# Six raw weight buffers, modulation tiles loaded one ahead, and half of layer 0's w_in multiplied without a split

## The chip, the core and the metric

The kernel runs on one core of a Trainium2 chip. TensorE (PE, with its weight loads listed as PEld) does the matrix products, VectorE (DVE), ScalarE (ACT) and GpSimd (POOL) the rest, and SyncE (SP) issues nearly all transfers from HBM. The metric is the device time of one execution in microseconds, the median over several runs.

## What is computed

Two layers of an encoder over 256 tokens of 2048 features, all in float32. Only what bears on the change is shown:

```
c_act = silu(c)                                   # (1, 2048)
for l in range(2):
    mod = c_act @ ada_w[l] + ada_b[l]             # 6 parts of 2048: sh1 sc1 g1 sh2 sc2 g2
    h = rmsnorm(x, norm_mix_g[l]) * (1 + sc1) + sh1
    proj = h @ w_in[l] + b_in[l]                  # 2048 -> 5392
    y = concat(RG-LRU, attention, hyena, mLSTM of slices of proj)
    x = x + g1 * (y @ w_out[l])                   # 2048 -> 2048
    h = rmsnorm(x, norm_ffn_g[l]) * (1 + sc2) + sh2
    x = x + g2 * ((silu(h @ ffn_w1[l]) * (h @ ffn_w3[l])) @ ffn_w2[l])   # 2048 -> 5632 -> 2048
return rmsnorm(x, final_g)
```

## The kernel before

Features lie on partitions, tokens on the free axis: the stream `x` is 16 row tiles of 128 features by 256 tokens. A weight matrix is read in *pieces* of 128 x 1024 floats (512 KB): four row tiles of a pair of 128-column blocks. w_in has 21 pairs, so 84 pieces, and 2 pieces more for the gates; w_out has 64, w1 and w3 together 176, w2 96 (some of 384 KB).

**Exact products out of fast passes.** The type F32R lets TensorE run a float32 product in one pass of reduced precision. To lose nothing, every weight piece and every activation tile is split into `hi` (ScalarE copies and rounds, L335) and `lo` (VectorE subtracts, L336), and `product` issues three matmuls per row tile and column block: hi by hi (L372), hi by lo (L373), lo by hi (L374). An activation tile `h` is made by `norm`'s `make(k)`: a tiny gain `g` (L493), `x` times gain times 1/rms (L495), the shift on ScalarE with rounding to hi (L497), and lo on VectorE (L498).

**Buffers.** `_load` brings pieces into `NRAW` = 3 raw tiles, `_split` makes `NHL` = 3 pairs of hi and lo. `fetch`, called ahead of each piece, loads and splits up to those numbers ahead of the piece in use. A raw tile is free again after its split.

**Modulation.** `mod` is a matrix-vector product that VectorE does: `ada` loads half a column block of ada_w (128 x 1024 floats, 512 KB) and multiplies and sums it in one instruction (L423), into `acc`; after the second half a tiny sum with the bias follows (L428, 128 x 1), or, for the parts g1 and g2, two for the whole part (L432, L433). There are 384 such halves. `RATES` says how many halves are worked on per weight piece: 1 in layer 0's w_in, less later, none after layer 1's w_out. `modc` computes on until a wanted column is there. The 64 halves that the first norm needs are worked through during the start, between the steps of `spectra` (the long filters of the hyena mixer, in full float32 products), with up to six tiles in flight; later halves have `NADA` = 2 tiles.

**Order.** A list scheduler orders the instructions of each engine at build time, from the program's order, priorities and its own timing; on the chip every engine and the SP queue run strictly in that order. `load` keeps a transfer behind the last weight load that the program asked for before it. The first `IN_LEAD` = 4 pairs of w_in are worked on together, chunk by chunk of four row tiles, as `h` comes into being; later pairs one after the other. The same holds for w_out (5 pairs) and w1/w3 (3 pairs).

Of the kernel before, what the change touches and what calls it, by code (L numbers as in the profile page):

```python
# [18 lines left out]
P = 128  # L19
DEPTH = 2  # L20
# [24 lines left out]
def _in_columns():  # L45
    """Source column of every column of the 42 plain blocks, in the kernel's order."""
# [33 lines left out]
# ---------------------------------------------------------------- constants of the shapes  # L80
def _constants():
# [36 lines left out]
    # behind the permutation of the rotation: rows 2 i and 2 i + 1 spread over the halves of tile i  # L118
# [38 lines left out]
# ---------------------------------------------------------------- layout of the inputs  # L157
# [67 lines left out]
# ---------------------------------------------------------------- the program  # L225
# pairs of column blocks that are worked on together while their input is still being made
IN_LEAD, OUT_LEAD, FFN_LEAD = 4, 5, 3
# half columns of the modulation per piece of weights, by layer: w_in, first w1 and w3, the rest of the FFN, w_out
# [3 lines left out]
class Lazy:  # L232
    """A list of n tiles, each made when it is first asked for, in their order."""
# [13 lines left out]
class Net:  # L247
    NRAW, NHL, NADA = 3, 3, 2
    # 2 KB tiles, by what they hold: a tag's tiles get their places in the order of the program
# [71 lines left out]
    def _load(self):  # L321
        ap, n = self.items[self.n_dma]
# [5 lines left out]
    def _split(self):  # L328
        k = self.n_split
        n = self.items[k][1]  # L330
        t = self.raw.pop(k)
        with self.tc.high_priority(offset=1500):
# [5 lines left out]
        self.n_split += 1  # L338
# [17 lines left out]
    def product(self, banks, acts, m):  # L356
        """bank[:, b*T:(b+1)*T] = W[:, block b].T @ act, for m blocks of 128 columns in each bank.
        acts: per row tile, [hi | lo]. Several banks take turns chunk by chunk."""
# [3 lines left out]
        for done in range(0, nk, per):  # L362
            use = [acts[done + i] for i in range(min(per, nk - done))]
            for ps in banks:
                hi, lo = self.next_weights()
                for i, a in enumerate(use):
                    for b in range(m):
# [3 lines left out]
                        last = done + i == nk - 1  # L371
                        mm(o, hi[:, c], a[:, :T], start=first and b == 0, stop=False, skip_group_check=True)  # L372
# [4 lines left out]
    def products(self, n, lead, acts):  # L377
        """The banks of n pairs of column blocks in turn; the first `lead` of them are worked on together."""
# [8 lines left out]
    def split(self, dst, src):  # L387
        """dst (float32r) = [hi | lo] of src, exactly."""
# [4 lines left out]
    def ada_init(self, order):  # L393
# [11 lines left out]
        self.acc = [self.cp.tile([P, 96, 2], F32, name=f"acc{l}") for l in range(DEPTH)]  # L405
        self.ada_items = [(l, b, h) for l, b in order for h in range(2)]
        self.ada_at = 0
        self.ada_left = 0.0

    def ada(self, n, wide=False):  # L410
        """The next n half columns of the modulation; wide: with more of them under way."""
        nc = self.nc
        self.ada_left += n
        while self.ada_left >= 0.999 and self.ada_at < len(self.ada_items):
            self.ada_left -= 1
            l, b, h = self.ada_items[self.ada_at]
            self.ada_at += 1
            if wide and self.ada_at % 3:
                t = self.pair("ad")
            else:  # L420
                t = self.wp.tile([P, 1024], F32, tag="ada", name=self.nm("ada"), bufs=self.NADA)
            self.load(t, self.d["ada"][l, b, :, h * 1024:(h + 1) * 1024])
            nc.vector.scalar_tensor_tensor(t, t, 1.0, self.cb[:, h * 1024:(h + 1) * 1024], ALU.mult, ALU.mult,  # L423
                                           accum_out=self.acc[l][:, b, h:h + 1])
            if h == 0:
                continue
            if b // 16 not in (2, 5):
                nc.vector.scalar_tensor_tensor(self.mod[l][:, b:b + 1], self.acc[l][:, b, 0:1], self.acc[l][:, b, 1:2],  # L428
                                               self.pc(l, "ada_b", b), ALU.add, ALU.add)
            elif b % 16 == 15:  # L430
                m = self.mod[l][:, b - 15:b + 1]
                nc.vector.tensor_tensor(m, self.acc[l][:, b - 15:b + 1, 0], self.acc[l][:, b - 15:b + 1, 1], ALU.add)  # L432
                nc.vector.tensor_tensor(m, m, self.pc(l, "ada_b", b - 15, 16), ALU.add)  # L433

    def modc(self, l, j, k):
        """Column k of part j; parts 2 and 5 come as a whole."""
        b = j * 16 + k
        while self.ada_at <= self.ada_items.index((l, b | 15 if j in (2, 5) else b, 1)):
            self.ada(1, wide=l == 0 and j < 2)
        return self.mod[l][:, b:b + 1]  # L440

# [1 line left out]
    def rsqrt(self, v, n):  # L443
        """v ** -0.5 of a tiny tile: a start from ScalarE, one Newton step on it."""
# [40 lines left out]
    def norm(self, l, gname, jsh, jsc):  # L485
# [3 lines left out]
        def make(k):  # L489
            sc, sh = self.modc(l, jsc, k), self.modc(l, jsh, k)  # L490
            with self.tc.high_priority(offset=50):
                g = self.yp.tile([P, 1], F32, tag="g", name=self.nm("g"))
                nc.vector.scalar_tensor_tensor(g, sc, 1.0, self.pc(l, gname, k), ALU.add, ALU.mult)  # L493
                t = self.tmp("h")
                nc.vector.scalar_tensor_tensor(t, self.x[k], g, rb, ALU.mult, ALU.mult)  # L495
                h = self.slot("h", F32R)
                nc.scalar.activation(h[:, :T], t, AF.Identity, bias=sh)  # L497
                nc.vector.scalar_tensor_tensor(h[:, T:], t, sh, h[:, :T].bitcast(F32), ALU.add, ALU.subtract)  # L498
# [13 lines left out]
    def sine(self, ps, b, sf):  # L512
        """sin(sf * (ps + b)) of 64 rows, the argument brought into [-pi, pi] first."""
# [16 lines left out]
    def filters(self):  # L530
        """The hidden layers of the networks of the long filters."""
# [13 lines left out]
    def spectra(self, h):  # L545
        """Spectra of the long filters, without their norm, into DRAM; the norms per channel into self.rs."""
# [13 lines left out]
    def third(self, l):  # L560
        """Last weights of the filters' network, the decays below those of the first quarter."""
# [7 lines left out]
    def early(self, n):  # L569
        """Modulation and first norm, between the steps of the spectra."""  # L570
        self.ada(min(n, 64 - self.ada_at), wide=True)
# [76 lines left out]
    def taps(self, src, dst, w, b, left):  # L648
        """Depthwise convolution over the tokens; w: columns of the taps."""
# [9 lines left out]
    def hyena(self, l, hf, pv, dft, spec, rs):  # L659
        """One half (two tiles) of the channels; pv: projections of v, x1, x2."""  # L660
# [58 lines left out]
    def attention(self, l, pq, pkv):  # L719
        """pq: two pairs of q tiles (heads i and i + 4 in tile i); pkv: k tile | v tile."""  # L720
# [395 lines left out]
    def weight_items(self):  # L1116
# [9 lines left out]
        def pairs(aps, lead, k0=0, k1=KT):  # L1126
            put(aps[:lead], k0, k1)
            for ap in aps[lead:]:
                put([ap], k0, k1)
# [58 lines left out]
```

## Time and profile before

| | |
|---|---|
| median of 3 runs | 2657.58 us (2656.99 to 2659.11) |
| span of the profiled execution | 2648.9 us; its own time is not listed, and the runs' times lie 8.1 to 10.2 us above this span |
| mean granted TensorE clock | 0.972 |
| PE busy | 2523.5 us (95%), 19410 matmul records |
| DVE busy | 1811.4 us (68%) |
| ACT busy | 1158.7 us (44%) |
| moved by DMA | 630.19 MB, mean 238 GB/s |

Times in the rows below are microseconds from the start of the span unless marked ns. A full float32 product appears as two weight loads and two matmul records, an F32R pass as one of each. Matmuls overlap in the pipeline, so what one costs is read from how closely the starts follow each other, not from its own length. Roughly, the start lasts until 175 us, layer 0's w_in with the mixers until 545, w_out until 627, the FFN until 1409; layer 1's w_in with the mixers until 1790, w_out until 1865, its FFN until 2636.

### The profile page before, as it was taken

How to read it: one execution, taken by the hardware profiler on the slowest of the kernel's cores; microseconds unless marked ns; L12 is line 12 of the kernel's file. 1: busy time of each engine (PE TensorE's matmuls, PEld its weight loads, DVE VectorE, ACT ScalarE, POOL GpSimd, SP SyncE). 2: the span in 40 equal slices, each digit the busy share in tenths (PEclk: the TensorE clock that was granted, in tenths of full speed). 3: DMA queues.
4: the chain of work that ended last, by engine and by line, in shares of the span. 5: the costliest groups of instructions: out<-in, count | busy, mean ns of one | idle time of the engine just before them, and what ended most of it. 6: DMA issues, size and time to landing. Idle time of an engine off the chain costs nothing.

```text
span 2648.9 us, 47579 instructions
## 1 busy us (share of the span) xinstructions
PE 2523.5 (95%) x19410; PEld 2404.3 (91%) x19410; DVE 1811.4 (68%) x2778; ACT 1158.7 (44%) x1669; POOL 161.9 (6%) x142
## 2 busy tenths in 40 slices
PE   6889989798999999999998999999899999999998
PEld 3469989598999999999998898989899999999998
DVE  7888788778767666766677767777766454454445
ACT  4444455444443344334434445654444334433443
POOL 2101010021000000000020111002000000000001
PEclk9789999898999999999999999999999999999999
DMA  8787878467887778887776766658688656556654
GB/s 281 267 308 267 263 255 295 173 244 241 278 281 272 263 267 266 271 265 269 254 257 231 254 219 229 212 167 271 223 282 270 192 183 183 180 181 189 183 180 148
DMA packets 180752, 630.19 MB, mean 238 GB/s; under 512 B 20162, under 2 KB 20371, under 8 KB 180531
## 3 DMA queue, kind: packets, MB, share of 16 engines
q1 hardware_dynamic: 177076, 620.84, 70.5%
q10 hardware_dynamic: 3456, 6.29, 0.6%
q8 instruction: 152, 2.49, 0.4%
q14 instruction: 68, 0.56, 0.1%
HBM read 618.67 MB, written 8.39 MB: 237 GB/s over the span
## 4 chain that ended last, share of the span: by engine, by line
PE 58%; DMA 8%; DVE 5%; issue 4%; ACT 1%; SPq 0%; POOL 0%; DVEq 0%; POOLq 0%; ACTq 0%
PE a L374 19%; PE a L373 19%; PE a L372 19%; DMA ada<-in_ada 6%; DVE lo L336 2%; DMA raw<-in_w_in 1%; DMA raw<-in_w 1%; DVE ada L423 1%; ACT hi L335 0%; DMA raw<-in_w_out 0%; DVE x L1097 0%; DVE h L495 0%; DVE h L498 0%; SPq L324 0%; PE m L812 0%
## 5 line engine op out<-in xcount | busy, mean ns | idle before, releaser
L335 ACT ACTIVATE hi<-raw 128x1024 fp32r<-128x1024 f32 (+2 forms) x780 | 810.8, 1041 | 1181.4 <-PE a L373 698.5
L336 DVE TENSOR_TENSOR lo<-raw,hi 128x1024 fp32r<-128x1024 f32 (+2 forms) x780 | 948.1, 1218 | 425.1 <-ACT hi L335 419.9
L374 PE MATMUL a<-h,lo 128*128 128x256 f32 x4192 | 1204.2, 288 | 26.7 <-DVE lo L336 26.6
L372 PE MATMUL a<-h,hi 128*128 128x256 f32 x4192 | 1206.0, 288 | 10.2 <-ACT hi L335 5.5
L373 PE MATMUL a<-h,hi 128*128 128x256 f32 x4192 | 1206.3, 288 | 1.7 <-DVE h L498 1.7
L374 PEld LDWEIGHTS a<-h,lo 128*128 128x128 f32 x4192 | 815.1, 195 | 40.6 <-DVE lo L336 30.2
L372 PEld LDWEIGHTS a<-h,hi 128*128 128x128 f32 x4192 | 815.7, 195 | 28.5 <-ACT hi L335 8.9
L373 PEld LDWEIGHTS a<-h,hi 128*128 128x128 f32 x4192 | 815.5, 195 | 8.1 <-DVE h L498 2.8
L423 DVE SCALAR_TENSOR_TENSOR ada<-ada,cb 128x1024 f32<-128x1024 f32 x341 | 425.1, 1247 | 340.7 <-DMA ada<-in_ada 339.9
L374 PE MATMUL a<-g,lo 128*128 128x256 f32 x1408 | 399.7, 284 | 2.9 <-DVE lo L336 2.8
L373 PE MATMUL a<-g,hi 128*128 128x256 f32 x1408 | 399.2, 283 | 0.0
L372 PE MATMUL a<-g,hi 128*128 128x256 f32 x1408 | 399.1, 283 | 0.0
L374 PEld LDWEIGHTS a<-g,lo 128*128 128x128 f32 x1408 | 271.0, 193 | 4.0 <-DVE lo L336 4.0
L372 PEld LDWEIGHTS a<-g,hi 128*128 128x128 f32 x1408 | 271.1, 193 | 0.0
L373 PEld LDWEIGHTS a<-g,hi 128*128 128x128 f32 x1408 | 271.0, 192 | 0.0
L466 POOL TENSOR_TENSOR sq<-sq,sq 128x256 f32<-128x256 f32 x65 | 81.6, 1255 | 1694.4 <-issue 1399.7
L1097 DVE SCALAR_TENSOR_TENSOR x<-a,mod,x 128x256 f32<-128x256 f32 x128 | 55.8, 477 | 5.5 <-PE a L374 5.4
L423 DVE SCALAR_TENSOR_TENSOR ad<-ad,cb 128x1024 f32<-128x1024 f32 x43 | 54.5, 1274 | 0.1
L389 ACT ACTIVATE g<-s 128x256 fp32r<-128x256 f32 x88 | 35.9, 408 | 35.2 <-DVE s L1109 35.1
L497 ACT ACTIVATE h<-h,mod 128x256 fp32r<-128x256 f32 x64 | 29.4, 501 | 42.0 <-DVE h L495 28.5
L464 ACT ACTIVATE sq<-x 128x256 f32<-128x256 f32 x75 | 29.2, 413 | 24.5 <-DVE x L1097 24.3
L374 PE MATMUL a<-yc,lo 128*128 128x256 f32 x128 | 36.8, 288 | 1.0 <-DVE lo L336 1.0
(247 smaller groups left out, 2017.7 us busy)
## 6 DMA issues: line engine op xcount, KB each, us to landing
raw<-in_w SPq DMA_DIRECT2D x496, 512.0 KB, 4.6
ada<-in_ada SPq DMA_DIRECT2D x341, 512.0 KB, 5.7
raw<-in_w_in SPq DMA_DIRECT2D x168, 512.0 KB, 4.9
raw<-in_w_out SPq DMA_DIRECT2D x64, 512.0 KB, 5.7
ad<-in_ada SPq DMA_DIRECT2D x43, 512.0 KB, 6.3
raw<-in_w SPq DMA_DIRECT2D x32, 384.0 KB, 3.1
spectra<-sl ACTq DMA_DIRECT2D x24, 256.0 KB, 7.0
spec<-spectra SPq DMA_DIRECT2D x24, 256.0 KB, 6.7
```

Of the source, the lines that this page charges most:

```text
L335: self.nc.scalar.activation(hi[:, :n], t[:, :n], AF.Copy)
L336: self.nc.vector.tensor_tensor(lo[:, :n], t[:, :n], hi[:, :n].bitcast(F32), ALU.subtract)
L372: mm(o, hi[:, c], a[:, :T], start=first and b == 0, stop=False, skip_group_check=True)
L373: mm(o, hi[:, c], a[:, T:], start=False, stop=False, skip_group_check=True)
L374: mm(o, lo[:, c], a[:, :T], start=False, stop=last, skip_group_check=True)
L389: self.nc.scalar.activation(dst[:, :T], src, AF.Copy)
L423: nc.vector.scalar_tensor_tensor(t, t, 1.0, self.cb[:, h * 1024:(h + 1) * 1024], ALU.mult, ALU.mult, accum_out=self.acc[l][:, b, h:h + 1])
L464: nc.scalar.activation(t, self.x[k], AF.Square)
L466: nc.gpsimd.tensor_tensor(self.sq, self.sq, t, ALU.add)
L497: nc.scalar.activation(h[:, :T], t, AF.Identity, bias=sh)
L1097: self.nc.vector.scalar_tensor_tensor(self.x[k], ps[:, b * T:(b + 1) * T], g, self.x[k], ALU.mult, ALU.add)
```

## The change

- `NRAW` goes from 3 to 6. Room is made by a smaller scratch for dynamic DMAs (`dynamic_dma_scratch_size=1024`).
- `WHOLE = 8`: in layer 0, row tiles 0 to 7 of w_in and of the gates are neither split nor is their `h`: `_split` hands on the raw tile, `make` leaves `h` as plain float32 without `lo`, and `product` issues one full float32 matmul in place of three passes. That is 42 of 84 pieces and 1 of 2 for the gates. Such a raw tile is held until its matmuls are done.
- `ada` no longer loads its own half: `ada_load` asks for the tiles ahead of the one that is summed, six in the first 58 halves, `NADA` = 2 (this one and the next) after that.
- The sums with the bias are made per part (two instructions of 128 x 16) and not per column, but for the first norm; the gain `(1 + sc) * norm_g` is made beside them into a kept tile, so `make` no longer computes `g`. For this the parts come one after the other in `order`, not column by column in turn, but for the first norm.

```
-    NRAW, NHL, NADA = 3, 3, 2
+    NRAW, NHL, NADA = 6, 3, 2
+WHOLE = 8
 def _split(self):
+        self.n_split += 1
+        if whole:
+            self.hl[k] = (t, None)
+            return
 def product(self, banks, acts, m):
+                        if lo is None:
+                            mm(o, hi[:, c], a[:, :T], start=first and b == 0, stop=last, skip_group_check=True)
+                            continue
+    def ada_load(self):
+        at = self.ada_at
+        while self.ada_got < min(len(self.ada_items), at + (6 if at < 58 else self.NADA)):
+            n = self.ada_got
+            l, b, h = self.ada_items[n]
+            if n < 64 and n % 3:
+                t = self.pair("ad")
+            else:
+                t = self.wp.tile([P, 1024], F32, tag="ada", name=self.nm("ada"), bufs=self.NADA)
+            self.load(t, self.d["ada"][l, b, :, h * 1024:(h + 1) * 1024])
+            self.ada_tiles[n] = t
+            self.ada_got += 1
 def ada(self, n):
+            self.ada_load()
             l, b, h = self.ada_items[self.ada_at]
+            t = self.ada_tiles.pop(self.ada_at)
...
+            if l == 0 and j < 2:
+                m = mod[:, b:b + 1]
+                nc.vector.scalar_tensor_tensor(m, acc[:, b, 0:1], acc[:, b, 1:2], self.pc(l, "ada_b", b), ALU.add, ALU.add)
+                if j:
+                    nc.vector.scalar_tensor_tensor(self.gain[l, j][:, k:k + 1], m, 1.0, self.pc(l, "nmix", k), ALU.add, ALU.mult)
+            elif k == 15:
+                c = slice(j * 16, j * 16 + 16)
+                nc.vector.tensor_tensor(mod[:, c], acc[:, c, 0], acc[:, c, 1], ALU.add)
+                nc.vector.tensor_tensor(mod[:, c], mod[:, c], self.pc(l, "ada_b", j * 16, 16), ALU.add)
+                if j in (1, 4):
+                    nc.vector.scalar_tensor_tensor(self.gain[l, j], mod[:, c], 1.0, self.pc(l, "nmix" if j == 1 else "nffn", 0, 16),
+                                                   ALU.add, ALU.mult)
 def make(k):   # in norm
-            sc, sh = self.modc(l, jsc, k), self.modc(l, jsh, k)
+            g, sh = self.modc(l, jsc, k), self.modc(l, jsh, k)
+            whole = l == 0 and jsh == 0 and k < WHOLE
-                nc.vector.scalar_tensor_tensor(g, sc, 1.0, self.pc(l, gname, k), ALU.add, ALU.mult)
-                h = self.slot("h", F32R)
+                h = self.slot("h", F32 if whole else F32R)
                 nc.scalar.activation(h[:, :T], t, AF.Identity, bias=sh)
+                if not whole:
+                    nc.vector.scalar_tensor_tensor(h[:, T:], t, sh, h[:, :T].bitcast(F32), ALU.add, ALU.subtract)
-        order = [(l, j * 16 + k) for l in range(DEPTH) for js in ((1, 0), (2,), (4, 3), (5,)) for k in range(16) for j in js]
+        order = [(0, j * 16 + k) for k in range(16) for j in (1, 0)]
+        order += [(l, j * 16 + k) for l in range(DEPTH) for j in ((1, 0) if l else ()) + (2, 4, 3, 5) for k in range(16)]
-    nc = bacc.Bacc("TRN2", target_bir_lowering=False, num_devices=1)
+    nc = bacc.Bacc("TRN2", target_bir_lowering=False, num_devices=1, dynamic_dma_scratch_size=1024)
```

## Rows read from the trace of the kernel before

**Rows 1.** Windows by stage: length, busy us (instructions) per engine, granted clock, DMA share, GB/s.

```profile
50.00:175.00 125.00, 112.07 (x395) 66.65 (x395) 112.47 (x222) 52.18 (x105) 21.09 (x12) 0.85 0.83 297
175.00:500.00 325.00, 298.89 (x2195) 283.96 (x2195) 266.22 (x461) 159.19 (x259) 24.64 (x26) 0.96 0.80 271
...
650.00:1345.00 695.00, 694.13 (x5782) 693.73 (x5782) 477.24 (x648) 284.52 (x339) 4.28 (x3) 1.00 0.80 270
...
1425.00:1790.00 365.00, 349.54 (x2590) 326.71 (x2590) 267.26 (x470) 191.02 (x328) 27.42 (x28) 0.98 0.67 221
...
1884.00:2636.00 752.00, 751.25 (x6262) 751.17 (x6262) 406.15 (x470) 309.51 (x373) 14.47 (x13) 1.00 0.64 202
```

**Rows 2.** Waits of TensorE, 175 to 500 us: us in total, times, longest.

```profile
PE a L374 <- DVE lo L336: 16.1, 7, 7.7
```

**Rows 3.** Waits of TensorE, 1340 to 1900 us.

```profile
PE a L374 <- DVE lo L336: 10.5, 9, 3.4
PE ss L475 <- ACT sq L464: 8.4, 2, 4.8
...
PE a L372 <- ACT hi L335: 2.3, 2, 1.8
```

**Rows 4.** One window of the dense stretch of layer 0's FFN.

```profile
900.00:1000.00 100.00, 100.00 (x836) 100.00 (x835) 67.55 (x96) 42.20 (x51) 0.00 (x0) 1.00 0.81 275
```

**Rows 5.** Timeline of TensorE in layer 1's hyena: start us, us, engine, line, op, tiles, form.

```profile
1513.07 3.62 PE L684 MATMUL m<-vt,dft 128*128 128x256 f32 x16
...
1516.64 0.28 PE L372 MATMUL a<-h,hi 128*128 128x256 f32 x1
```

**Rows 6.** Windows of L374 alone: PE busy us (records), PEld busy (records), clock.

```profile
0.00:175.00 175.00, 29.05 (x84) 20.20 (x84) 0.89 0.83 291
```

**Rows 7.** Groups of VectorE, 50 to 175 us: busy us, mean ns, idle before.

```profile
L423 DVE SCALAR_TENSOR_TENSOR ad<-ad,cb 128x1024 f32<-128x1024 f32 x35 | 44.9, 1288 | 0.1
...
L336 DVE TENSOR_TENSOR lo<-raw,hi 128x1024 fp32r<-128x1024 f32 x9 | 11.7, 1297 | 3.3 <-ACT hi L335 3.3
...
L498 DVE SCALAR_TENSOR_TENSOR h<-h,mod,h 128x256 fp32r<-128x256 f32 x13 | 6.7, 516 | 4.9 <-ACT h L497 4.9
```

**Rows 8.** Groups of the whole span, by shape: VectorE.

```profile
L336 DVE TENSOR_TENSOR lo<-raw,hi 128x1024 fp32r<-128x1024 f32 x732 | 901.5, 1233 | 394.5 <-ACT hi L335 389.4 <-PE a L373 0.7 <-PE a L374 0.5
...
L428 DVE SCALAR_TENSOR_TENSOR mod<-acc,par 128x1 f32<-128x1 f32 x128 | 32.2, 252 | 1.4
...
L493 DVE SCALAR_TENSOR_TENSOR g<-mod,par 128x1 f32<-128x1 f32 x64 | 11.1, 178 | 0.3
```

**Rows 9.** Windows around three slow stretches, columns as in the first group.

```profile
182.00:190.00 8.00, 6.17 (x30) 6.17 (x31) 5.85 (x9) 1.46 (x2) 0.00 (x0) 0.57 0.52 143
353.00:364.00 11.00, 5.75 (x28) 5.75 (x29) 11.00 (x16) 2.39 (x4) 4.28 (x4) 0.53 0.40 117
...
1613.00:1624.00 11.00, 7.20 (x35) 6.79 (x35) 11.00 (x13) 2.86 (x5) 3.82 (x3) 0.53 0.36 104
```

**Rows 10.** Waits of the SP queue, whole span.

```profile
SPq L324 <- DVE lo L336: 1332.6, 574, 43.9
```

**Rows 11.** Waits of VectorE, 175 to 500 us.

```profile
DVE ada L423 <- DMA ada<-in_ada: 48.2, 36, 2.9
```

**Rows 12.** Waits of ScalarE, 590 to 627 us, the end of layer 0's w_out.

```profile
ACT hi L335 <- DMA raw<-in_w: 6.2, 3, 4.4
```

**Rows 13.** Waits of ScalarE, 1396 to 1409 us, the end of layer 0's FFN.

```profile
ACT hi L335 <- DMA raw<-in_w_in: 4.3, 2, 2.8
```

**Rows 14.** Waits of ScalarE, 1850 to 1865 us, the end of layer 1's w_out.

```profile
ACT hi L335 <- DMA raw<-in_w: 6.1, 3, 2.8
```

**Rows 15.** Waits of TensorE, 545 to 650 us.

```profile
PE ss L475 <- ACT sq L464: 3.5, 1, 3.5
```

**Rows 16.** The two DMA queues that carry data: packets, MB, share of 16 engines.

```profile
q1 hardware_dynamic: 177076, 620.84, 70.5%
q10 hardware_dynamic: 3456, 6.29, 0.6%
```

More of the change, by code (lines that the diff above doesn't have):

```diff
@@ L321, in _load @@
     def _load(self):
-        ap, n = self.items[self.n_dma]
+        ap, n, _ = self.items[self.n_dma]
         t = self.wp.tile([P, 1024], F32, tag="raw", name=self.nm("raw"), bufs=self.NRAW)
@@ L329, in _split @@
         k = self.n_split
-        n = self.items[k][1]
+        n, whole = self.items[k][1:]
         t = self.raw.pop(k)
+        self.n_split += 1
+        if whole:
+            self.hl[k] = (t, None)
+            return
         with self.tc.high_priority(offset=1500):
@@ L337, in _split @@
         self.hl[k] = (hi, lo)
-        self.n_split += 1
     def fetch(self):
@@ L405, in ada_init, with ada @@
         self.acc = [self.cp.tile([P, 96, 2], F32, name=f"acc{l}") for l in range(DEPTH)]
+        self.gain = {(l, j): self.cp.tile([P, 16], F32, name=f"gain{l}{j}") for l in range(DEPTH) for j in (1, 4)}
         self.ada_items = [(l, b, h) for l, b in order for h in range(2)]
-        self.ada_at = 0
+        self.ada_at = self.ada_got = 0
         self.ada_left = 0.0
-    def ada(self, n, wide=False):
+        self.ada_tiles = {}
+    def ada_load(self):
[10 more added lines that the diff above has]
+            self.ada_got += 1
+    def ada(self, n):
         nc = self.nc
@@ L415, in ada @@
             self.ada_left -= 1
+            self.ada_load()
             l, b, h = self.ada_items[self.ada_at]
+            t = self.ada_tiles.pop(self.ada_at)
             self.ada_at += 1
[L418 to L422, printed above, removed]
+            acc, mod = self.acc[l], self.mod[l]
@@ L423, in ada @@
             nc.vector.scalar_tensor_tensor(t, t, 1.0, self.cb[:, h * 1024:(h + 1) * 1024], ALU.mult, ALU.mult,
-                                           accum_out=self.acc[l][:, b, h:h + 1])
+                                           accum_out=acc[:, b, h:h + 1])
+            j, k = b // 16, b % 16
             if h == 0:
                 continue
[L427 to L433, printed above, removed]
+            if l == 0 and j < 2:
[10 more added lines that the diff above has]
+                                                   ALU.add, ALU.mult)
@@ L435, in modc @@
     def modc(self, l, j, k):
         b = j * 16 + k
-        while self.ada_at <= self.ada_items.index((l, b | 15 if j in (2, 5) else b, 1)):
-            self.ada(1, wide=l == 0 and j < 2)
-        return self.mod[l][:, b:b + 1]
+        while self.ada_at <= self.ada_items.index((l, b if l == 0 and j < 2 else b | 15, 1)):
+            self.ada(1)
+        return self.gain[l, j][:, k:k + 1] if j in (1, 4) else self.mod[l][:, b:b + 1]
     def rsqrt(self, v, n):
@@ L483, in rstd, with norm @@
         return pb[:, :T]
-    def norm(self, l, gname, jsh, jsc):
+    def norm(self, l, jsh, jsc):
         nc = self.nc
@@ L569, in early @@
     def early(self, n):
-        self.ada(min(n, 64 - self.ada_at), wide=True)
+        self.ada(min(n, 64 - self.ada_at))
         k = min(self.ada_at // 4, KT)
@@ L1118, in weight_items, with put @@
         d, it = self.d, []
-        def put(aps, k0, k1, w=256):
+        def put(aps, k0, k1, w=256, whole=0):
             per = 1024 // w
@@ L1123, in put, with pairs @@
                 n = min(per, k1 - k)
-                it.extend((ap[:, k:k + n, :].rearrange("p a b -> p (a b)"), n * w) for ap in aps)
-        def pairs(aps, lead, k0=0, k1=KT):
-            put(aps[:lead], k0, k1)
+                it.extend((ap[:, k:k + n, :].rearrange("p a b -> p (a b)"), n * w, k < whole) for ap in aps)
+        def pairs(aps, lead, k0=0, k1=KT, whole=0):
+            put(aps[:lead], k0, k1, whole=whole)
             for ap in aps[lead:]:
-                put([ap], k0, k1)
+                put([ap], k0, k1, whole=whole)
         for l in range(DEPTH):
             w = [d["w_in"][l, j] for j in range(21)]
-            pairs(w[:14], IN_LEAD)
-            put([d["w_gate"][l]], 0, KT, P)
-            pairs(w[14:], 1)
+            whole = 0 if l else WHOLE
+            pairs(w[:14], IN_LEAD, whole=whole)
+            put([d["w_gate"][l]], 0, KT, P, whole=whole)
+            pairs(w[14:], 1, whole=whole)
             pairs([d["w_out"][l, j] for j in range(8)], OUT_LEAD)
@@ L1153, in run @@
         self.weights(self.weight_items())
-        self.ada(4, wide=True)
-        self.h0 = h = self.norm(0, "nmix", 0, 1)
+        self.ada(4)
+        self.h0 = h = self.norm(0, 0, 1)
         self.early(4)
@@ L1161, in run @@
         for l in range(DEPTH):
-            h = h or self.norm(l, "nmix", 0, 1)
+            h = h or self.norm(l, 0, 1)
             self.rate = RATES[l][0] if l else 0
@@ L1166, in run @@
             self.add_to_stream(l, y, 2, True, OUT_LEAD)
-            h = self.norm(l, "nffn", 3, 4)
+            h = self.norm(l, 3, 4)
             self.ffn(l, h)
```

2 lines of the change are left out of this document (removed).

## Prediction, made before the changed kernel was run

> **What bounds the kernel now.** I read the windows by stage first. In both FFN stretches TensorE is busy all the time at full clock (694.1 of 695 us, 751.3 of 752), so 1447 us are bound by matmuls alone and nothing that the change does to VectorE or to transfers can shorten them. The rest is where time can come from: the start, layer 0's w_in, the norms between matrices, and layer 1's w_in and w_out [rows 1]. The busy share of TensorE flatters these stages, since a matmul that waits in the pipeline is counted. The count tells more: 2195 records in the 325 us from 175 to 500. Then I read TensorE's own waits by stage. In layer 0's w_in the largest wait is for lo, the second half of the weight split on VectorE: 16.1 us in 7 waits [rows 2]. In the 560 us around layer 1's mixer it is 10.5 us for lo and 2.3 for hi, and 8.4 us at two norms for the squares of the last row of the stream [rows 3]. VectorE is busy for 266 of those 325 us and 112 of 125 in the start [rows 1]: near full, so its queue is late whenever something else falls in.
>
> **The added cost: the unsplit products.** In the dense FFN 836 F32R passes start in 100 us, 0.1196 us each [rows 4]; a split row tile and column block is three of them, 0.359 us. A full float32 product of the same shape (128 rows, 128 columns, 256 moving) is in the hyena: sixteen records, eight products, start at 1513.07, and one F32R pass later the next start is at 1516.64; 3.57 less 0.12 is 3.45 us, 0.431 us each [rows 5]. So an unsplit product costs 0.072 us more than the three passes it replaces. There are 43 such pieces of 8 products, 344 in all: 24.9 us of TensorE time added. L374 has run 84 of its 688 times for layer 0's w_in by 175 us [rows 6], and the first eight pieces, which are all unsplit, are 64 of these: so 4.6 us fall into the start and 35 pieces, 20.3 us, into the dense part. Bounds of one product: 0.359, if it costs no more than the three passes, and 0.453, the eighth part of the 3.62 us from the first start to the last end [rows 5]; over 344 products nothing and 32 us.
>
> The Trainium skill has a rule that speaks against the change here: the page FP8 and Floating Point Precision, section TensorE Precision Notes, says that a true float32 product is four passes through the array. At the pass spacing of the FFN, weight load included, that would make 0.478 us a product and 41 us in all, and the sum below would be some 16 us higher. The row in the hyena gives 0.431, and the measurement decides.
>
> **What it removes, in the start.** VectorE no longer makes lo of eight pieces (1.297 us each, 10.4) and of eight tiles of h (0.516, 4.1) [rows 7]: 14.5 us off an engine that is busy 112 of 125 us. It stands idle for only 0.1 us before the sums on tiles of the modulation there, so it is not the loads that pace it. But TensorE also waits for the spectra and runs at a mean clock of 0.85 [rows 1], and its 4.6 us more are partly in the way. Bounds: 14.5 gained, 4.6 lost; I take 7 gained, about the middle of 14.5 and 0.
>
> **In layer 0's w_in.** Half of the pieces need neither ScalarE nor VectorE, 1.233 us of VectorE each [rows 8], 43 us of its 266. What that returns is at most the 16.1 us of waits for lo and the clock that they cost. In two windows with such waits the granted clock is 0.57 and 0.53, with 6.2 and 5.8 us busy: times the missing share, 2.7 us lost in each [rows 9]. That makes 21.5. I take 16, three quarters: the longest wait (7.7) stands behind the recurrences of the RG-LRU on VectorE's queue, which stay. Against the 20.3 us added this stage comes out 4 us longer; bounds 1 shorter and 20 longer.
>
> **Six raw buffers.** SP waits 1332.6 us for lo before it can load a piece [rows 10]: with three buffers a load goes out only once an older piece is split. Three more let each load go out three pieces earlier, 72 passes or some 8.6 us [rows 4]. In the FFN this is worth nothing. At the norms it counts: shortly before the last rows of the stream, ScalarE waits 6.2, 4.3 and 6.1 us for the next weights [rows 12 to 14], VectorE's queue stands behind it with lo, and the last update of x and its square come late; TensorE waits 3.5 and 8.4 us for them [rows 3, 15], 11.9 in all. I take 8 for the three norms; bounds 0 and 11.9. In layer 1's stages the waits for lo and hi are 12.8 us, and a half-clock window with 7.2 us busy lost 3.4 [rows 3, 9]: 16.2 at most. Some of them are queued behind activations of the recurrence and not behind loads, so I take 9; bounds 0 and 16.2.
>
> An unsplit raw tile is held until its matmuls are done, three pieces later than a split would free it; the three added buffers just pay for that. Queued behind such a load on SP are the next modulation tile and the tables of the mixers; who waits for them is VectorE, not TensorE. I cost it at nothing; without that cover it is a longer wait of VectorE of the kind that already costs 2.9 us at worst [rows 11].
>
> **Modulation loads and sums.** After the start there are two tiles for the modulation before and after, so a load still waits for the sum of two halves earlier: I expect most of VectorE's 48.2 us of waits for these tiles to stay [rows 11], and give the earlier request nothing. Removed are 96 of the 128 tiny sums with the bias (0.252 us) and 48 of the 64 gains made at their places (0.178), 33 us of VectorE [rows 8]; the 12 wide sums and three wide gains that replace them are a few us. What lies in the FFN stretches gains nothing; at the norms a tiny gain sits ahead of each of the first tiles, half a us, inside the 8 taken above. The first norm's sums stay single. The smaller scratch I cost at nothing: all data go through the two queues listed, both of the hardware kind, the same that the loads use now [rows 16]. No transfer's size or number changes.
>
> **The sum.** -7 (start) +4 (layer 0's w_in) -8 (three norms) -9 (layer 1) = -20 us against the span of 2648.9, so 2629; the median of the runs lies 8.7 above the span, which gives 2638 us. A change within 0.2%, 5.3 us, can't be told from none.
>
> **The rivals.**
> *Slower: the waits stay.* VectorE's and ScalarE's backlog in layer 0's w_in comes from the mixers, and the removed splits only leave VectorE idle. TensorE then pays the 24.9 us in full in that one stage, with the 8 of the norms returned: 2675 us. For it: waits for lo are only 16.1 of the 325 us [rows 2], and wherever there is none an unsplit product is pure loss. Against it: those waits are for the very work that is removed. It decides once less than about 20 us is recovered over the whole kernel.
> *More than forecast.* VectorE was the bound of the start after all, and the deeper loads remove every weight wait: -14.5, -1, -12, -16, together -44, 2614 us. For it: VectorE 90% busy in the start. Against: stalls behind the recurrences are not of the weights' making.
> *It comes out even.* Either an unsplit product costs four passes at the spacing of the FFN, 0.478 us and 16 us more in all than I take: 2654; the row of the hyena speaks against it, and it gets 0.05. Or the change doesn't do what it says: the earlier loads leave the splits where they were, since VectorE and not the loads set them, and of the 17 us at the norms and in layer 1 hardly any come: about 2655, with 0.09. (The rule of the Trainium skill named above is the first of these two.)
>
> **How the numbers follow.** Chances: the forecast 0.50 (its own range 2620 to 2652), more than forecast 0.20, even 0.14, slower 0.16. So faster 0.70, the same 0.14, slower 0.16. The range must hold 8 in 10: it reaches below to a little past the 2614 of the second rival and above close to the 2675 of the first, 2608 to 2672.
>
> **What would show it.** In the trace of the changed kernel: records of float32 products on `a<-h,raw` at 0.216 us spacing, 688 of them; L336 with 43 fewer groups of work; the lead pieces of w_in done some 7 us sooner; TensorE's waits for lo in layer 0's w_in down from 16 to about 4 us while that stage takes as long as before; ScalarE's waits for weights before the three norms gone, and the wait for the last square short; the FFN stretches unchanged. Wrong would be: an unsplit product at another spacing, a clock below 0.96 in w_in, or VectorE waiting longer than now for modulation tiles with TensorE behind it.

## The result

| | before | after |
|---|---|---|
| median on the same chip, 4 runs each | 2657.87 us (2656.99 to 2659.11) | 2639.76 us (2636.45 to 2642.18) |
| ratio, 95% interval | | 0.9933 [0.9917, 0.9950] |
| profiled execution: time, span | not listed, 2648.9 us | 2639.2 us, 2637.4 us |
| mean granted TensorE clock | 0.972 | 0.981 |

The change saves 18 us, where 20 were forecast. The profiled execution of after shows that a run's time lies only 1.8 us above its span. A second profile of before says the same (2660.62 and 2658.8). So the execution behind [rows 1 to 16] took about 2650.7 us, 7 below its kernel's median, and the 8.7 us that the prediction added were mostly this difference. Counted between medians the sum is not hurt; a stage read from that one execution is. The second profile of after errs the other way: its execution took 2652.61 us, the slowest of its six and 11 above their median.

The stages can be compared by the matmul `rb<-ident,v`, which starts each norm. Timeline of TensorE in after (start us, us, engine, line, op, tiles, form; in brackets the idle time before it):

```profile
29.59 0.69 PE L511 MATMUL rb<-ident,v 128*128 128x128 f32 x2 [4.04 <-DMA dft<-in_k_dft]
...
619.61 0.69 PE L511 MATMUL rb<-ident,v 128*128 128x128 f32 x2 [1.04 <-POOL v L508]
...
1407.51 0.69 PE L511 MATMUL rb<-ident,v 128*128 128x128 f32 x2 [2.37 <-POOL v L508]
...
1857.00 0.69 PE L511 MATMUL rb<-ident,v 128*128 128x128 f32 x2 [3.31 <-POOL v L508]
...
2626.87 0.43 PE L511 MATMUL rb<-ident,v 128*128 128x128 f32 x2 [1.03 <-POOL v L508]
```

The same rows of the second profile of before:

```profile
628.65 0.69 PE L482 MATMUL rb<-ident,v 128*128 128x128 f32 x2 [2.35 <-POOL v L479]
...
1419.13 0.69 PE L482 MATMUL rb<-ident,v 128*128 128x128 f32 x2 [1.85 <-POOL v L479]
...
1876.69 0.69 PE L482 MATMUL rb<-ident,v 128*128 128x128 f32 x2 [1.41 <-POOL v L479]
```

One more mark is the start of the last matmul of the 128th product of w_in, as many as the four pairs that are worked on together have; the time up to it is here called the *lead*. (In after, 7 of the 128 are already of the fifth pair, which the scheduler put ahead.) With it the span falls into stages, in us (two executions of each kernel):

| | lead | rest to the first FFN norm | layer 0's FFN | layer 1 to its FFN norm | layer 1's FFN |
|---|---|---|---|---|---|
| before | 197.6, 195.7 | 433.5, 432.9 | 781.0, 790.5 | 455.6, 457.6 | 770.4, 771.6 |
| after | 188.7, 189.1 | 430.9, 432.8 | 787.9, 785.1 | 449.5, 460.2 | 769.9, 773.0 |

Only the lead shows a difference that is larger than that between two executions of one kernel. Layer 0's FFN alone differs by 9.5 us between the two of before. The lead's difference is 8 us of the 18; by stage, the other 10 can't be told from the spread of these four executions.

The unsplit products are there, 688 records. The groups of after by line, TensorE:

```profile
L378 PE MATMUL a<-h,raw 128*128 128x256 f32 x688 | 166.6, 394 | 3.9 <-DMA raw<-in_w_in 3.9
```

128 of them lie before 175 us, the 64 products that the prediction put there. Windows of L378 alone (length, PE busy (records), PEld busy (records), clock, DMA share, GB/s):

```profile
0.00:175.00 175.00, 37.54 (x128) 27.87 (x128) 0.90 0.87 308
```

Their price is in the timeline of TensorE in after:

```profile
263.00 0.28 PE L382 MATMUL a<-h,lo 128*128 128x256 f32 x1
263.12 4.05 PE L378 MATMUL a<-h,raw 128*128 128x256 f32 x18
267.01 0.60 PE L704 MATMUL m<-ident,hn 128*128 128x128 f32 x4
```

18 records, nine products, start between 263.12 and 267.01: 0.216 us a record, 0.432 a product, as [rows 5] had it. The Trainium skill's four passes (FP8 and Floating Point Precision, TensorE Precision Notes) are in it if a pass is taken at a quarter of this, 0.108 us. The prediction's 0.478 by that rule came from taking each pass at the 0.1196 us of [rows 4]; the trace is against that price, not against the number of passes.

VectorE's splits, by shape, have 43 fewer large groups than in [rows 8]:

```profile
L342 DVE TENSOR_TENSOR lo<-raw,hi 128x1024 fp32r<-128x1024 f32 x689 | 849.5, 1238 | 348.4 <-ACT hi L341 345.1
```

Windows by stage, as in [rows 1]: from 175 to 500 VectorE is busy for 220 us, not 266.

```profile
50.00:175.00 125.00, 113.02 (x385) 66.77 (x385) 111.99 (x223) 50.13 (x102) 21.93 (x11) 0.86 0.89 318
175.00:500.00 325.00, 301.76 (x1790) 267.91 (x1790) 220.22 (x403) 121.26 (x235) 27.34 (x28) 0.97 0.74 253
```

Waits of TensorE, 175 to 500 us (total, times, longest). The 16.1 us for lo of [rows 2] are 0.9 now. What is left waits mostly for the mixers:

```profile
PE m L860 <- DVE lf L858: 8.3, 1, 8.3
PE a L380 <- ACT h L525: 3.0, 1, 3.0
...
PE a L382 <- DVE lo L342: 0.9, 1, 0.9
```

So lo was taken out of the way, but TensorE's idle time in this stretch, the length less the busy time, only went from 26.1 us [rows 1] to 23.2. The longest wait that came up, 8.3 us, stands behind a late weight piece. ScalarE, which takes its work strictly in order, waits 6.3 us for the piece and only then computes `ga`, from which VectorE makes `lf`:

```profile
376.85 1.06 ACT L341 ACTIVATE hi<-raw 128x1024 fp32r<-128x1024 f32 x1 [6.32 <-DMA raw<-in_w_in]
...
380.95 0.42 ACT L857 ACTIVATE ga<-ga 128x256 f32<-128x256 f32 x1
...
381.39 0.42 DVE L858 SCALAR_TENSOR_TENSOR lf<-gates,ga 128x256 f32<-128x256 f32 x1 [2.23 <-ACT ga L857]
...
381.88 1.11 PE L860 MATMUL m<-lf,ident 64*64 64x256 f32 x2 [8.31 <-DVE lf L858]
```

VectorE's waits for modulation tiles in the same stretch grew from the 48.2 us of [rows 11]:

```profile
DVE ada L446 <- DMA ada<-in_ada: 78.9, 49, 4.1
```

TensorE stands behind a few of them: its waits of 2.7 and 1.9 us for the hyena's `hn` come right after such a tile. The prediction had named this as a sign of being wrong. Timeline of after at the first of the two:

```profile
297.50 1.23 DVE L446 SCALAR_TENSOR_TENSOR ada<-ada,cb 128x1024 f32<-128x1024 f32 x1 [2.63 <-DMA ada<-in_ada]
...
298.65 0.48 DVE L737 SCALAR_TENSOR_TENSOR hn<-m,c,hn 128x256 f32<-128x256 f32 x1
...
299.18 0.70 PE L1029 MATMUL m<-xc,lw 128*128 128x256 f32 x2 [2.72 <-DVE hn L737]
```

### The profile page after: what moved, and what is told of

It is laid out like the page before. It is cut to its first block, busy times and chain, and to the rows that moved or that the text cites. A ratio compares the mean times of both kernels' runs of the same rounds, so it can differ in the third digit from the quotient of the medians.

```text
span 2637.4 us, 46636 instructions
## 1 busy us (share of the span) xinstructions
PE 2524.1 (96%) x19066; PEld 2393.4 (91%) x19066; DVE 1739.9 (66%) x2598; ACT 1117.8 (42%) x1626; POOL 158.8 (6%) x142
## 5 line engine op out<-in xcount | busy, mean ns | idle before, releaser
L341 ACT ACTIVATE hi<-raw 128x1024 fp32r<-128x1024 f32 (+2 forms) x737 | 765.2, 1040 | 1121.9 <-PE a L381 972.6
L342 DVE TENSOR_TENSOR lo<-raw,hi 128x1024 fp32r<-128x1024 f32 (+2 forms) x737 | 895.0, 1221 | 377.6 <-ACT hi L341 374.3
L380 PE MATMUL a<-h,hi 128*128 128x256 f32 x3848 | 1104.7, 288 | 10.2 <-ACT h L525 6.6
L382 PE MATMUL a<-h,lo 128*128 128x256 f32 x3848 | 1099.9, 286 | 9.8 <-DVE lo L342 9.7
L381 PE MATMUL a<-h,hi 128*128 128x256 f32 x3848 | 1100.5, 286 | 1.5 <-DVE h L527 1.5
L380 PEld LDWEIGHTS a<-h,hi 128*128 128x128 f32 x3848 | 743.2, 193 | 17.9 <-ACT h L525 8.0
L382 PEld LDWEIGHTS a<-h,lo 128*128 128x128 f32 x3848 | 742.9, 193 | 18.0 <-DVE lo L342 12.4
L381 PEld LDWEIGHTS a<-h,hi 128*128 128x128 f32 x3848 | 743.6, 193 | 7.9 <-issue 3.4
L446 DVE SCALAR_TENSOR_TENSOR ada<-ada,cb 128x1024 f32<-128x1024 f32 x342 | 428.2, 1252 | 444.4 <-DMA ada<-in_ada 443.9
L378 PE MATMUL a<-h,raw 128*128 128x256 f32 x688 | 166.6, 394 | 3.9 <-DMA raw<-in_w_in 3.9
L378 PEld LDWEIGHTS a<-h,raw 128*128 128x128 f32 x688 | 132.1, 197 | 34.0 <-issue 15.3
L446 DVE SCALAR_TENSOR_TENSOR ad<-ad,cb 128x1024 f32<-128x1024 f32 x42 | 52.8, 1265 | 0.7 <-DMA ad<-in_ada 0.7
```

Of the source, the lines that this page charges most:

```text
L341: self.nc.scalar.activation(hi[:, :n], t[:, :n], AF.Copy)
L342: self.nc.vector.tensor_tensor(lo[:, :n], t[:, :n], hi[:, :n].bitcast(F32), ALU.subtract)
L378: mm(o, hi[:, c], a[:, :T], start=first and b == 0, stop=last, skip_group_check=True)
L381: mm(o, hi[:, c], a[:, T:], start=False, stop=False, skip_group_check=True)
L382: mm(o, lo[:, c], a[:, :T], start=False, stop=last, skip_group_check=True)
```

## The experiments

Ratios are to before on the same chip; edits are to the changed kernel unless another is named. Each edit also makes the scheduler order the instructions anew; no run holds that order fixed, so a part of any difference may be the new order. Stage lengths come from one profiled execution of each run.

**1 to 4: the parts one by one.**

```
e1:  WHOLE = 0
e2:  NRAW, NHL, NADA = 3, 3, 2
e3:  WHOLE = 0;  NRAW, NHL, NADA = 3, 3, 2
e4:  the kernel before, with NRAW = 6 and dynamic_dma_scratch_size=1024
```

> The change without unsplit products (WHOLE = 0): six raw buffers, modulation asked for ahead, sums per part. My theory: the start is 9 us longer again, as VectorE makes lo of eight pieces and eight tiles of h there, and layer 0's w_in loses the 20 us of added matmul time but gets its 16 us of waits for lo back, so about 2650 us. Rival, the unsplit products bring nothing on balance: within 5 us of the changed kernel, 2635 to 2645.

> The change with three raw buffers (NRAW = 3). My theory: raw buffers are what shortens the norms and layer 1's stages, so 10 to 17 us of that is lost there; in layer 0's w_in an unsplit tile is held until its matmuls are done, so loads go out late and TensorE waits for them: 2655 to 2670 us. Rival, the deeper loads cost as much at the FFN (7 us of waits behind late modulation tiles) as they bring: about 2640 us, with the FFN of layer 0 back at 781 us between its norms.

> Only the modulation part of the change (NRAW = 3, WHOLE = 0): asked for one tile ahead, sums and gains per part, parts in turn. My theory: worth nothing, 2655 to 2660 us, the waits of VectorE for modulation tiles near the 340 us of the kernel before, layer 0's FFN between its norms at 781 us. Rival: the waits of VectorE that hold up TensorE in layer 0's FFN in the changed kernel come from this part; then the FFN is some 7 us longer here too, and the whole 2660 to 2667 us; or the tiny sums taken from the norms are worth their 33 us of VectorE in part, 2645 to 2652.

> The kernel before with six raw buffers and the smaller scratch alone. My theory: the norms and layer 1's stages gain 10 to 17 us and layer 0's FFN loses some 7 us, since each modulation load is kept behind weight loads that now stand three pieces further ahead: 2645 to 2655 us, with VectorE waiting over 400 us for modulation tiles. Rival: the FFN's loss belongs to the new order of modulation loads; then no loss here, FFN 781 us, 2640 to 2648 us.

| | ratio | median, us |
|---|---|---|
| e1, all but the unsplit products | 0.9952 [0.9934, 0.9970] | 2647.13 |
| e2, all but the six buffers | 1.0063 [1.0041, 1.0086] | 2674.85 |
| e3, the modulation part alone, with the smaller scratch | 1.0007 [0.9991, 1.0023] | 2659.40 |
| e4, six buffers alone | 0.9961 [0.9948, 0.9975] | 2648.23 |

The times of e1, e3 and e4 lie where the theories had them; e2 is 5 us above its range. What they said of layer 0's FFN did not hold: it takes 786.4 us in e3, where 781 were expected, and 782.1 in e4, where 788 were.

The modulation part is worth nothing (e3, and e1 beside e4). The buffers alone give 10 us (0.39% of 2658). The unsplit products give another 5 to 7 on top of them (0.9952 against 0.9933, and 0.9925 in experiment 5), but cost 15 us when there are only three buffers (0.56%, e2 against e3). There the stage behind the lead takes 456.1 us against e3's 435.1, while the lead is shorter (192.8 against 197.4). Waits of ScalarE from 175 to 650 us, in e2 and then in e3:

```profile
ACT hi L341 <- DMA raw<-in_w_in: 147.4, 29, 10.8
```

```profile
ACT hi L341 <- DMA raw<-in_w_in: 20.8, 17, 3.7
```

With three buffers, tiles held until their matmuls are done make the loads of the pieces that are still split late: 147 us of waiting, where e3, which splits every piece, has 21. In after, with six buffers, it is 23.6, and one of these waits is the one behind which TensorE stood for 8.3 us. So the added buffers pay for most of the tiles held, and what the unsplit products give hangs on them.

**5 and 6: both kernels again**, with no edit: after with 6 runs, before with one profiled execution.

> The changed kernel unaltered, to see how far its stages move from one execution to another. My theory: layer 0's FFN between its norms again takes some 788 us, 5 to 7 more than before the change, with VectorE waiting over 400 us for modulation tiles; 2635 to 2645 us. Rival: that stage was long by chance, and is at 781 us here.

> The kernel before unaltered, one more profile beside this chip's runs. My theory: its span is 2 us below its own time, so about 2656, and the profile on which the prediction rested, with a span of 2648.9, was of a fast execution; the stages are within 3 us each of that profile. Rival: the time around the span is 9 us, and the span is 2649 again.

After: 0.9925 [0.9911, 0.9938], median 2641.37 us (2636.89 to 2652.61). Before's profiled execution took 2660.62. The difference stands, and so does the spread: 11 runs of before beside them had a median of 2661.28. Before's span is 1.8 us below its time, as the theory had it, but its stages are not within 3 us of the first profile. I had held the late modulation tiles to cost 7 us in layer 0's FFN, since after's 787.9 us there stood against 781.0. The second profile of before refutes it: 790.5, with waits of TensorE for lo from 640 to 1400 us as long as in after (8.9 us from 640 to 1395).

```profile
PE a L374 <- DVE lo L336: 9.7, 10, 3.3
```

**7: a third tile for the modulation.**

```
-    NRAW, NHL, NADA = 6, 3, 2
+    NRAW, NHL, NADA = 6, 3, 3
```

> The changed kernel with a third tile for the modulation after the start (NADA = 3, and loads up to two ahead). My theory: the waits of VectorE for these tiles (444 us in the changed kernel) are what holds up TensorE in layer 0's FFN; they fall below 200 us, the FFN of layer 0 returns to about 781 us between its norms and 5 to 10 us are gained: 2629 to 2636 us. Rival: those waits cost nothing, since TensorE is fed anyway: 2637 to 2643.

0.9957 [0.9945, 0.9968], 2649.20 us: not a gain, but a loss of 6 to 9 us against after. VectorE's waits for these tiles stayed (443.9 us in after), layer 0's FFN took 785.9 us, and the lead 196.9, which is 8 us longer. Waits of VectorE over the span of this run, then TensorE's from 0 to 200 us:

```profile
DVE ada L446 <- DMA ada<-in_ada: 461.4, 268, 6.7
```

```profile
PE a L380 <- ACT h L525: 11.1, 4, 6.0
```

The expectation fell. Depth in tiles is not what keeps these loads late. Why the start grew is open; in it TensorE waits for `h`. The edit was not confined to the time after the start, as every third of the first 64 tiles comes from the same buffers.

**8, 9 and 11: how far the trade goes.** e8 leaves all 16 row tiles of layer 0 unsplit, e9 those of both layers, and e11 is e8 with a seventh buffer.

```
e8:   WHOLE = 16
e9:   WHOLE = 16;  whole = jsh == 0 and k < WHOLE (in make);  whole = WHOLE (in the items of w_in)
e11:  WHOLE = 16;  NRAW, NHL, NADA = 7, 3, 2
```

> All 16 row tiles of layer 0's w_in unsplit (WHOLE = 16). My theory: TensorE bounds layer 0's w_in once half of the pieces are unsplit, as its waits for lo there are down to 0.9 us; 43 more pieces cost 0.58 us each, 25 us, of which the start hides some 5 and gives back a few: 2650 to 2662 us. Rival: VectorE is still the bound there, and freeing it more is worth the added matmul time: at most 2642.

> w_in unsplit in both layers, all 16 row tiles. My theory after the run with all of layer 0 unsplit: added matmul time is free as long as the mixers' work on VectorE leaves TensorE idle in the same stage; in layer 0 the idle time there fell from 63 to 44 to 29 us while 40 us of matmuls were added. Layer 1's mixer stage has some 42 us of idle time, of which 20 stand at its norms and in the wait for the recurrence; 50 us of matmuls are added, so that stage gets some 25 to 35 us longer: 2660 to 2675 us. Rival, freeing VectorE pays the same way in layer 1: about 2638 us again.

> All of layer 0's w_in unsplit, with seven raw buffers. My theory: six are enough, since a weight load leaves five pieces ahead of its use and ScalarE's waits for weights are gone already: within 4 us of the run with all unsplit, 2634 to 2642. Rival: unsplit tiles, held until their matmuls are done, still starve the loads in layer 0; then its stage from the lead pieces to the second norm is 5 to 10 us shorter.

e8: 0.9911 [0.9899, 0.9924], 2637.96 us. My theory that all unsplit would be slower fell, and its rival had the time right: another 25 us of matmuls cost nothing. e9: 1.0025 [1.0011, 1.0038], 2667.24 us. Layer 1 then takes 481.7 us to its FFN norm, 28 more than in e8; its 688 unsplit products at 0.072 us add 50, so not half of the added work is recovered there, as the theory expected. In layer 0 the same 50 us are recovered whole: lead and rest are 627.8 us in e1 and 621.4 in e8. e11: 0.9905 [0.9886, 0.9925], 2635.64 us, as its theory had it: the lowest median of all, but not to be told from e8, and neither clearly from after (0.9925 [0.9911, 0.9938]).

The windows of e8 show what changed. VectorE's time from 175 to 500 us falls to 177 us, the granted clock is 1.00 there, and 0.95 in the start, where after has 0.86:

```profile
50.00:175.00 125.00, 117.47 (x354) 68.47 (x353) 106.02 (x213) 43.54 (x96) 19.42 (x12) 0.95 0.86 307
175.00:500.00 325.00, 319.13 (x1518) 270.60 (x1517) 177.37 (x370) 89.66 (x211) 25.62 (x28) 1.00 0.74 250
```

An estimate of the slack: the matmuls of the stage behind the lead, counted by kind in the trace and each taken at the closest spacing of its kind, need 366.8 us in e1, 386.6 in after and 407.5 in e8. What is left of the stage is 63.0, 44.3 and 28.8 us. So the slack takes up 18.7 of the first 19.8 us added and 15.5 of the next 20.9, and the lead, 198.0, 188.7 and 185.1 us, gives back 9.3 and 3.6, over both steps more than the rest. In layer 1 the stage, its lead included, needs 412.8 us with every piece split and has 37 to 47 us left in after's two profiles, where layer 0 had 63.0 without its lead. In e9 some 19 us are left; why no more of it can be bought is open.

**10: modulation loads set free.** e8, with the modulation tile's load no longer kept behind the weights.

```
-            self.load(t, self.d["ada"][l, b, :, h * 1024:(h + 1) * 1024])
+            self.nc.sync.dma_start(t, self.d["ada"][l, b, :, h * 1024:(h + 1) * 1024])
```

> All of layer 0's w_in unsplit, and loads of the modulation no longer kept behind the weight loads asked for before them. My theory: VectorE's waits for modulation tiles (444 to 507 us) come from their loads standing behind weight loads on SP; free, they fall below 250 us, and the few waits of TensorE for lo in the FFN go with them: 2628 to 2637 us. Rival: two tiles are two tiles, a load can't leave before its tile is free, the waits stay over 400 us and the time is that of the run with all unsplit, 2634 to 2642.

1.0113 [1.0089, 1.0137], 2689.71 us, 52 slower than e8, and outside what either theory gave. VectorE's waits for the tiles did fall:

```profile
DVE ada L446 <- DMA ada<-in_ada: 294.1, 216, 7.0
```

But VectorE then took in sums earlier, and more of them ahead of layer 0's FFN. Windows of L446 alone (VectorE busy (records, two to a sum), clock, DMA share, GB/s), first e8, then e10, each for the stage behind the lead and for layer 1 up to its FFN norm:

```profile
185.14:621.44 436.30, 121.46 (x193) 1.00 0.77 259
1402.74:1856.38 453.64, 81.50 (x128) 0.98 0.67 226
```

```profile
179.20:693.20 514.00, 193.41 (x308) 0.93 0.82 278
1468.99:1904.13 435.14, 0.00 (x0) 0.99 0.50 159
```

In e10, 72 us more of sums stand in VectorE's queue among the mixers of layer 0, and the stage behind the lead grows by 78, from 436.3 to 514.0 us. TensorE's waits in e10, 180 to 700 us, are for the mixers; the same three make up 2.9 us in e8:

```profile
PE m L833 <- DVE pe L827: 17.1, 5, 5.7
PE m L732 <- POOL ta L723: 11.5, 3, 5.5
PE m L860 <- DVE lf L858: 7.8, 1, 7.8
```

The late loads had held VectorE's sums back, to the good of layer 0's mixers. What e10 moved forward it saved later: with no sum left in it, layer 1's stage is 18.5 us shorter than in e8, and layer 0's FFN takes 775.8 us, less than in any other profile here (781.0 to 792.6). The waits named are some 34 us of the 78; that the rest also follows from the sums is likely by their size, not shown.

**12: unsplit products, but the splits made all the same.** The hi and lo of the unsplit pieces and the lo of their `h` are computed and thrown away; TensorE multiplies as in after.

```
 def _split(self):
-        if whole:
-            self.hl[k] = (t, None)
-            return
...
-        self.hl[k] = (hi, lo)
+        self.hl[k] = (t, None) if whole else (hi, lo)
 def make(k):
-                if not whole:
-                    nc.vector.scalar_tensor_tensor(h[:, T:], t, sh, h[:, :T].bitcast(F32), ALU.add, ALU.subtract)
+                nc.vector.scalar_tensor_tensor(h[:, T:], t, sh, h[:, :T].bitcast(F32), ALU.add, ALU.subtract)
```

> The changed kernel with its unsplit products, but the 43 unsplit pieces and the 8 tiles of h are split as before and the parts thrown away: TensorE pays the 25 us more and VectorE and ScalarE are not relieved. My theory, VectorE's relief is what takes the idle time out of the start and of layer 0's w_in: the start is back at 196 us or more, w_in keeps some 60 us of idle time on top of its longer matmuls, 2655 to 2672 us. Rival, the longer matmuls merely fill time in which TensorE was kept waiting anyway by modulation tiles and mixers: about 2641 us, as the changed kernel.

1.0001 [0.9983, 1.0019], 2660.28 us. All of the gain is gone, that of the buffers too. The lead takes 197.3 us, after's 188.7, and the stage behind it 441.8 against 430.9. So, but for what the new order of instructions may do, the relief of the two engines that split is the mechanism, worth some 18 to 20 us: without it the unsplit products cost 13 (1.0001 against e1's 0.9952), with it they return 5 to 7. How much of it is VectorE's share and how much ScalarE's this run doesn't tell, since it gives both their work back.

## Why the prediction came out right, and where it did not

The total was right, at -18 us of a forecast -20, but that it came so close is in part luck. The unsplit products gave 5 to 7 us where the first two terms together forecast 3, the buffers 10 to 13 where the next two forecast 17, and the two misses partly cancel. By stage:

| term | forecast | measured | by |
|---|---|---|---|
| start | -7 | -9 | lead 198.0 in e1, 188.7 in after |
| unsplit products behind it | +4 | +1 to +3 | 429.8 in e1, 430.9 and 432.8 in after |
| three norms | -8 | about -1, not clear of nothing | waits below |
| layer 1 | -9 | about -2 to -3, less than executions differ | 455.6 and 457.6 before, 454.0 in e4, 454.6 in e1, 449.5 and 460.2 in after |
| modulation, scratch | 0 | 0 | e3; e1 beside e4 |

**The unsplit products** went by the mechanism that was named. Their number, price and place are as forecast, e12 shows that relief is what pays, and both terms lie within their bounds. The rival that the waits stay, which needed less than 20 us recovered over the whole kernel, is out: 24.9 us were added, and the time fell. Only the source of the recovery was drawn wrongly: I allowed at most 21.5 us, the waits for lo and their clock. The waits for lo went, but others came in their place, and TensorE's idle time from 175 to 500 us fell by only 3 us while its stage took up the added matmuls. Experiment 8 recovers more still. So the slack in this stage is not only what stands in a wait for lo; what the rest of it consists of, these rows don't say. One late piece has 8.3 us of TensorE's waiting behind it in after, 8.5 in its second profile and 2.4 in e8. Whether holding the unsplit tiles, which I had costed at nothing, made that piece late, no run shows.

**Six raw buffers** give 10 to 13 us (e4, e1), not 17, and hardly at the places named. The waits of ScalarE for weights did go. Over the span of before's second profile:

```profile
ACT hi L335 <- DMA raw<-in_w: 365.7, 200, 4.4
ACT hi L335 <- DMA raw<-in_w_in: 73.2, 39, 4.6
ACT hi L335 <- DMA raw<-in_w_out: 41.0, 21, 3.5
```

Of these the list of after has one:

```profile
ACT hi L341 <- DMA raw<-in_w_in: 23.6, 5, 14.0
```

The step that failed is "VectorE's queue stands behind it with lo, and the last update of x and its square come late". At the three norms TensorE's wait for the last square went from 11.9 us [rows 3, 15], 10.7 in before's second profile, only to 3.4 + 4.5 + 1.4 = 9.3 and 10.0 in after's two, and to 10.0 in e4; in e3, with three buffers, it is 9.4. The timeline of after at the end of layer 0's FFN shows what stands there in place of the weights (SP's and the weight-load rows left out):

```profile
1398.28 0.28 PE L382 MATMUL a<-g,lo 128*128 128x256 f32 x1
...
1400.08 1.22 DVE L446 SCALAR_TENSOR_TENSOR ada<-ada,cb 128x1024 f32<-128x1024 f32 x1 [2.77 <-DMA ada<-in_ada]
1401.23 0.08 DVE L446 DVE_READ_ACCUMULATOR ada<-ada,cb 128x1 f32 x1
1401.23 1.22 DVE L342 TENSOR_TENSOR lo<-raw,hi 128x1024 fp32r<-128x1024 f32 x1
1402.37 0.87 DVE L1126 SCALAR_TENSOR_TENSOR x<-a,mod,x 128x256 f32<-128x256 f32 x2
...
1402.94 0.81 ACT L493 ACTIVATE sq<-x 128x256 f32<-128x256 f32 x2 [3.40 <-DVE x L1126]
...
1403.41 1.73 PE L504 MATMUL ss<-misc,sq 128*128 128x1 f32 x8 [4.51 <-ACT sq L493]
```

The last product starts at 1398.28. VectorE stands idle until a modulation tile has landed (2.77 us), sums it, subtracts one lo, and comes to x only at 1402.37. In before the same sum stood there, and VectorE waited 2.70 us for the tile (1.80 in the second profile), while ScalarE was waiting for weights on its own queue. Of two late inputs I had named one and removed it; the other was enough to keep the wait. At the norm after layer 0's w_out a sum stands ahead of the update of x as well (idle 1.31 us), and at layer 1's it stands ahead of the row of rb (1.26 idle, then 1.23). Experiment 10 bears this out: its freed loads leave no tile late by more than 0.3 us just ahead of the update of x at any of the three norms, and TensorE's wait for the last square falls to a third. Its waits from 600 to 2000 us, in e8 and then in e10:

```profile
PE ss L504 <- ACT sq L493: 11.0, 3, 5.3
```

```profile
PE ss L504 <- ACT sq L493: 3.6, 3, 1.4
```

With the wait for rb, which comes next, TensorE's waits at the three norms are 15.8 us in e8 and 9.3 in e10. So some 6 us of the 8 forecast for the norms were there to be had, but by the modulation's loads and not by the weights'. Moving the sum behind x and rb by itself was not tried.

**Layer 1** was over-sized in the same way. The 12.8 us of waits for lo and hi were read from 1340 to 1900 us, which takes in the end of layer 0's FFN; in layer 1's own stages, from 1425 to 1860, they are 8.9 us in before and 9.1 in its second profile, 6.6 in e4, 6.9 and 9.5 in after's two. So at most 2.5 us of them went. Loads come earlier; that the lo that is waited for stands in VectorE's queue behind other work is argued, not shown.

**Not placed.** That six buffers give 10 us is shown by the medians of e4 and before; where they give it is open for the greater part. The stage behind the lead is 4 us shorter in the two runs with six buffers and every piece split (429.2 in e4, 429.8 in e1) than in the three profiles with three (433.5, 432.9, and 435.1 in e3), while their lead is 1 to 2 us longer. In e4 layer 0's FFN is about 4 us shorter than before's mean (785.8 and 782.1) and layer 1 about 2.6, both less than two executions of a kernel differ by. The prediction held both FFN stretches to be bound by matmuls alone; that layer 0's takes 781.0 and 790.5 us in two profiles of before and 775.8 in e10 shows some time there that is not.

## What to carry to other kernels

An operation that is slower on the busy engine can pay if it takes work off the engines that feed it, as long as that stage has slack; the slack is what remains of the stage after the matmuls are counted, and it has to be tested stage by stage, since layer 0 took up all of the added matmuls and layer 1 less than half. When a wait has two late inputs in one strict queue, relief for one of them alone can leave the wait nearly whole: read the whole queue ahead of the late instruction, not only the longest wait in it. Take two profiles before a stage's length from one is trusted to a few microseconds.

## What the runs showed of the hardware

- Executions of one kernel differ more than I took them to: before ranged from 2646.88 to 2664.68 us in 26 runs beside experiment 1, and layer 0's FFN, the same instructions, took 781.0 and 790.5 us in two profiles.
- From 50 to 175 us the mean granted clock was 0.86 in after, with TensorE busy for 113.0 us, and 0.95 in e8, with 117.5; from 175 to 500 us it was 0.97 with 301.8 us busy and 1.00 with 319.1.
- A full float32 product of 128 x 128 weights and 256 columns takes 0.432 us from start to start, three F32R passes 0.359.
- Loads kept behind others on one queue can make a kernel faster: letting them go ahead cost 52 us (e10 beside e8).
